# Attention in pairs of heads: row halves for the scores, column halves for the values

## The chip, the cores and the metric

The kernel runs on one core of a Trainium2 chip, in one launch. A core has a matrix engine (TensorE; PE in the profile, its weight loads PEld), a vector engine (VectorE, DVE), a scalar engine (ScalarE, ACT), a general one (GpSimd, POOL) and a queue engine for DMA (SyncE, SP). Each engine works off its own list of instructions in order, and semaphores hold one back until another is done. The metric is the device time of one launch in microseconds, the median of three runs.

## The reference, cut to what matters

Two transformer blocks on 256 tokens of 1024 features, in float32. The first block has two layers, each an attention mixer and a feed-forward part (dense, then eight experts); the second block has one mixer and one feed-forward part. The attention of all four kinds has this core:

```python
s = einsum('hqd,hkd->hqk', q, k) * scale + bias      # scores
m = s.max(-1); e = exp(s - m); den = e.sum(-1)        # softmax; windowed heads add exp(sink - m)
o = einsum('hqk,hkd->hqd', e / den, v)                # values
```

Layer 0 has 8 neighbourhood heads of 64 features (256 latent queries over 512 keys, with a bias; 256 context queries over 256 keys). Layer 1 has 8 windowed heads of 64 (256 queries, 512 keys, two value groups) and 4 differential heads of two halves each. The second block has 4 dilated heads (256 queries, three groups of 256 keys) and 8 MLA heads (96 features for the scores, 64 for the values). Beside layer 0's mixer, modulation vectors are computed: a vector of 1024 times a matrix, for two streams.

## The kernel before, in words

Every matrix of weights streams from HBM and is split by ScalarE (L213) and VectorE (L214) into two parts (`wh`, `wl`), so that a product of full precision is three fast ones (L231 to L233). The attention's own products take float32 operands as they are, and the profile shows each of them as two records.

The program is written out instruction by instruction. A stage's `main` is a generator that issues the projections step by step; each head (or tile of queries of a head) is a task, another generator, with a `yield` after each of its steps. `drive` (L284) sets the order: in a round it issues one step of `main`, starts tasks from `pend` at a rate, lets every live task do one step, and in layer 0 issues `pace` steps of the modulation sums (`ada`, L482: a load of `araw`, then VectorE's L508 or L510 for either stream, and after eight of them TensorE's L522 or L532). A round in which `main` must wait still does the rest. Tiles are shared through `Res` (L62): a task that finds none free yields until one is put back. The eight PSUM banks go through `Bank` (L89), a kind of use each: BG projections, BS scores, BT transposes, BO outputs, with a largest number and a number kept free. So the order on every engine is what these counts make of it.

A task of layer 0 (`head_task`, L785) is one head and one tile t of queries (t 0 and 1 are 128 latent queries each, t 2 both context tiles): load the bias (GpSimd's DMA queue), one score product into a bank (64 rows of the array, the half where the head's features lie), VectorE adds the bias and takes the maximum, ScalarE's Exp sums as it goes, TensorE transposes four blocks of 128, ScalarE or VectorE in turn copies them out, and the value products have the transposed probabilities as stationary side and 64 value columns as moving side, so that the output has tokens on the partitions. When all six tasks of a pair of heads are done, VectorE divides by the denominators and four transposes bring the output to features. The projections of the pairs (`pair_unit`) share two `qkv` tiles (L712): a third pair's projection is copied out (L748) once the first pair's six tasks have ended.

`win_task` (L1319), `dil_task` (L1935) and `mla_task` (L1998) do the same, with one bank for scores (two in `dil_task`) and `merged` (L542) for division and transposes. `diff_task` (L1387) already computes two scores, on the two row halves.

## Time and profile before

| | |
|---|---|
| median of 3 runs | 1788.38 us (1785.85 to 1791.57) |
| span of the profiled execution | 1782.2 us (the profile shows no time outside it; the median lies 6.2 above) |
| TensorE busy | 1686.3 us, 95% |
| weight loads | 1409.1 us, 79% |
| VectorE busy | 1285.6 us, 72% |
| ScalarE busy | 879.4 us, 49% |
| mean granted TensorE clock | 0.984 |
| layer 0's mixer, attention | 108 to 277 us |
| layer 1's mixer, attention | 774 to 877 us |
| second block's mixer, attention | 1414 to 1544 us |

Busy time is the union of the instructions' recorded spans. A product's record includes the latency through the array, which overlaps with the next record; how long it keeps the engine is the distance to the next start.

### The profile page before, as it was taken

To read this page: it belongs to the slowest core of one execution; us is meant where nothing else is said; L and a number is where in the kernel's file an instruction comes from. 1 tells how busy PE (TensorE), PEld (TensorE's weight loads), DVE (VectorE), ACT (ScalarE), POOL (GpSimd) and SP (SyncE) were. 2 spreads that over 40 slices of the span, in tenths; PEclk is the share of its full clock that TensorE was granted. 3 is DMA by queue.
4 is the path that set the end of the run, shared out by engine and by line. 5 is a ranking of instruction groups with operands and counts; after the bars stand their busy time and mean duration, and the time that the engine had idled before them with its cause. 6 is when DMAs were issued, how large, how long until landed. Compare 5 with 4: busy or idle time off the path is not lost. (4 is left out here: it accounts for less than half of the span.)

```text
span 1782.2 us, 23176 instructions
## 1 busy us (share of the span) xinstructions
PE 1686.3 (95%) x8894; PEld 1409.1 (79%) x8894; DVE 1285.6 (72%) x1892; ACT 879.4 (49%) x1326; POOL 75.8 (4%) x149
## 2 busy tenths in 40 slices
PE   5999999999999999999879999999997999979998
PEld 4787877887888887766658888788877999869997
DVE  5788755766765676787879899898996566575555
ACT  6533233522222223435557777777764466545443
POOL 1011100020000000000000000000000000000000
PEclk9998999999999999999999999999998999989999
DMA  8754422473555542343229989898975544246552
GB/s 270 214 163 132 160 71 71 141 204 116 164 181 191 177 142 82 132 142 119 81 80 363 346 298 346 300 359 308 356 233 159 173 131 130 84 141 202 189 189 95
DMA packets 182598, 331.21 MB, mean 186 GB/s; under 512 B 7614, under 2 KB 60192, under 8 KB 182480
## 3 DMA queue, kind: packets, MB, share of 16 engines
q1 hardware_dynamic: 167904, 279.73, 46.1%
q0 software_dynamic: 14576, 49.92, 9.2%
q8 instruction: 72, 1.18, 0.3%
q14 instruction: 46, 0.38, 0.1%
HBM read 328.57 MB, written 1.05 MB: 185 GB/s over the span
## 5 line engine op out<-in xcount | busy, mean ns | idle before, releaser
L214 DVE TENSOR_TENSOR wl<-raw,wh 128x1024 fp32r<-128x1024 f32 (+3 forms) x511 | 570.6, 1145 | 179.8 <-ACT wh L213 177.9
L213 ACT CAST wh<-raw 128x1024 fp32r<-128x1024 f32 (+3 forms) x511 | 489.3, 990 | 285.8 <-PE bank L233 169.7
L231 PE MATMUL bank<-aT,wh 128*128 128x512 f32 (+1 forms) x480 | 186.2, 388 | 1.3 <-DVE aT L435 0.9
L232 PE MATMUL bank<-aT,wh 128*128 128x512 f32 (+1 forms) x480 | 183.1, 381 | 0.8 <-DVE aT L436 0.6
L233 PE MATMUL bank<-aT,wl 128*128 128x512 f32 (+1 forms) x480 | 182.5, 380 | 0.0
L510 DVE SCALAR_TENSOR_TENSOR acc<-araw,sT,acc 128x1024 f32<-128x1024 f32 x105 | 131.1, 1279 | 8.3 <-DMA araw<-in_ada_w_dram 8.1
L231 PE MATMUL bank<-wh,aT 128*128 128x512 f32 (+2 forms) x320 | 119.7, 374 | 5.4 <-DVE aT L435 3.9
L232 PE MATMUL bank<-wl,aT 128*128 128x512 f32 (+2 forms) x320 | 116.8, 365 | 2.8 <-DVE wl L214 2.8
L233 PE MATMUL bank<-wh,aT 128*128 128x512 f32 (+2 forms) x320 | 117.0, 366 | 0.2 <-DVE aT L436 0.2
L232 PE MATMUL bank<-wl,gh 128*128 128x512 f32 (+1 forms) x306 | 114.7, 375 | 2.7 <-DVE wl L214 2.6
L231 PE MATMUL bank<-wh,gh 128*128 128x512 f32 (+1 forms) x306 | 115.7, 378 | 0.0
L233 PE MATMUL bank<-wh,gl 128*128 128x512 f32 (+1 forms) x306 | 114.9, 375 | 0.0
L231 PEld LDWEIGHTS bank<-aT,wh 128*128 128x128 f32 x480 | 90.5, 189 | 23.2 <-ACT P L760 1.5
L232 PEld LDWEIGHTS bank<-aT,wh 128*128 128x128 f32 x480 | 90.6, 189 | 20.5 <-DVE aT L436 1.6
L233 PEld LDWEIGHTS bank<-aT,wl 128*128 128x128 f32 x480 | 90.5, 189 | 19.1
L231 PEld LDWEIGHTS bank<-wh,aT 128*128 128x128 f32 x320 | 61.6, 192 | 16.7 <-DVE aT L435 4.2
L231 PE MATMUL bank<-zT,wh 128*128 128x256 f32 x256 | 71.5, 279 | 0.0
L232 PE MATMUL bank<-zT,wh 128*128 128x256 f32 x256 | 71.3, 279 | 0.0
L233 PE MATMUL bank<-zT,wl 128*128 128x256 f32 x256 | 71.3, 278 | 0.0
L231 PE MATMUL bank<-wh,hidh 128*128 128x512 f32 x176 | 70.0, 398 | 0.0
L233 PE MATMUL bank<-wh,hidl 128*128 128x512 f32 x176 | 69.1, 393 | 0.9 <-DVE hidl L1109 0.9
L232 PEld LDWEIGHTS bank<-wl,aT 128*128 128x128 f32 x320 | 61.5, 192 | 10.5 <-DVE wl L214 3.7
(502 smaller groups left out, 3609.9 us busy)
## 6 DMA issues: line engine op xcount, KB each, us to landing
raw<-in_moe_w_dram SPq DMA_DIRECT2D x96, 1024.0 KB, 7.3
araw<-in_ada_w_dram POOLq DMA_DIRECT2D x80, 512.0 KB, 4.2
raw<-in_moe_w_dram SPq DMA_DIRECT2D x48, 768.0 KB, 5.8
raw<-in_w_ff_dram SPq DMA_DIRECT2D x32, 1024.0 KB, 5.6
raw<-in_ffn_w_dram SPq DMA_DIRECT2D x30, 1024.0 KB, 6.9
raw<-in_ev_w_in_dram SPq DMA_DIRECT2D x48, 256.0 KB, 4.4
raw<-in_w_in_dram SPq DMA_DIRECT2D x10, 1024.0 KB, 5.0
raw<-in_w_in_dram SPq DMA_DIRECT2D x12, 768.0 KB, 4.5
```

Source lines behind the costliest of these rows:

```text
L213: ACT.copy(out=h, in_=v)
L214: DVE.tensor_sub(out=l, in0=v, in1=h)
L231: PE.matmul(o, lt[0], rt[0], start=first, stop=False, skip_group_check=True)
L232: PE.matmul(o, lt[0], rt[1], start=False, stop=False, skip_group_check=True)
L233: PE.matmul(o, lt[1], rt[0], start=False, stop=last, skip_group_check=True)
L510: DVE.scalar_tensor_tensor(acc[s], r, sT[:, s, k:k + 1], acc[s], op0=OP.mult, op1=OP.add)
```

## The change

Two heads make one task. Their two score products are cut into pieces of 256 columns that alternate between the upper and the lower 64 rows (`halves`), into a bank each. For the values, the sides are exchanged: the values (64 columns) are stationary, head 0 on the left half of the columns and head 1 on the right half, and the transposed probabilities stream (`weighted`); the output has features on the partitions, two heads in one bank, and needs no transposes. Since the denominators belong to tokens, `divided` spreads their reciprocals over the features by a product with the identity, after ScalarE has copied the reciprocals out to 512 columns and the output out of its bank, and VectorE multiplies. Tasks take two score banks (four in `dil_task`), two tiles of probabilities and two of their transposes at once; the kept numbers of banks and the rates of `drive` follow; the bias of a pair comes in one load into one tile. `diff_task` uses `halves`. Everything else, the projections, the feed-forward parts and the number of transposes of probabilities among them, stays. (Comments went too; line numbers move by about ten.)

```diff
-    def merged(o, den, BO, rP, BT):
-        """o: two tiles of rows, each of four heads (tokens, (tile, head, 64)), den: their denominators ->
-        a bank of features: ((head, 64) of two heads, (which two, tile, token))"""
-        on = yield from rP.get()
+    def halves(s, q, k, n):
+        for c in range(0, n, 256):
+            for i in range(2):
+                PE.matmul(s[i][:, c:c + 256], q[sl(i, 64)], k[sl(i, 64), c:c + 256], start=True, stop=True)
+    def weighted(o, V, PT, blocks):
+        for n, kt in enumerate(blocks):
+            for i in range(2):
+                PE.matmul(o[sl(i, 64)], V(kt, i), PT(kt, i), start=(n == 0), stop=(n == len(blocks) - 1),
+                          skip_group_check=True)
+    def divided(o, den, y, BO, rP, BT):
+        rd = yield from rP.get()
+        rd = rd[:, 0:512]
         DVE.reciprocal(den, den)
-        DVE.tensor_mul(on[:, :512].rearrange("p (g d) -> p g d", d=64), o.rearrange("p (g d) -> p g d", d=64),
-                       den[:, :, None].to_broadcast([128, 8, 64]))
+        ACT.copy(out=rd.rearrange("p (g d) -> p g d", d=64), in_=den[:, :, None].to_broadcast([128, 8, 64]))
+        ACT.copy(out=y, in_=o)
         BO.put()
         yield
         b = yield from BT.get()
-        for a in range(2):
-            for t in range(2):
-                PE.transpose(b[:, a * 256 + t * 128:][:, :128], on[:, t * 256 + a * 128:][:, :128], ident)
+        for i in range(4):
+            PE.matmul(b[:, sl(i)], rd[:, sl(i)], ident, start=True, stop=True)
         rP.put()
         yield
-        return b
...
-        rP, rPT, rB = (Res(wk, n, k) for n, k in (("P", 4), ("PT", 2), ("bias", 2)))
-        rB.args = ([128, 256], F32)
+        rP, rPT, rB = (Res(wk, n, k) for n, k in (("P", 4), ("PT", 2), ("bias", 1)))
...
+            pend.extend(pair_task(p, t, qkv, QT, KT, ob) for t in range(3))
+        def pair_task(p, t, qkv, QT, KT, ob):
+            ctx_ = t == 2
+            o = yield from shared(ob, 0, BO)
+            if not ctx_:
+                bias = yield from rB.get()
+                bv = bias.rearrange("p (h k) -> p h k", h=2)
+                POOL.dma_start(out=bv, in_=A["rpb_t"][2 * p:2 * p + 2, t].rearrange("h q k -> q h k"))
+                yield
+            den = dens[p].rearrange("p (t h) -> p t h", h=2)
+            nm = yield from rS.get()
+            s = yield from BS.several(2)
+            if ctx_:
+                for i in range(2):
+                    for hh in range(2):
+                        rs = sl(hh, 64)
+                        PE.matmul(s[hh][:, sl(i, 256)], QT[rs, sl(2 + i)], KT[rs, 256:512], start=True, stop=True)
+            else:
+                halves(s, QT[:, sl(t)], KT, 512)
+            yield
+            P = yield from rP.several(2)
             for hh in range(2):
...
+            rS.put()
+            yield
+            PT = yield from rPT.several(2)
+            for hh in range(2):
...
+                return qkv[:, kt, 256 + i * 64:320 + i * 64]
+            if ctx_:
+                weighted(o[:, 256:512], V, lambda kt, i: PT[i][:, sl(kt - 2, 256)], (2, 3))
             else:
...
+                weighted(o[:, sl(t)], V, lambda kt, i: PT[i][:, sl(kt)], range(4))
+            rPT.put(2)
             done[p] += 1
-            if done[p] == 6:
+            if done[p] == 3:
...
+            if done[p] == 3:
...
+                yield from divided(o, dens[p], y32[:, 4 + p, :], BO, rP, BT)
                 done[p] = 7
...
-                    for kind in (BS, BT, BO):
-                        kind.kept = 1
+                    BS.kept, BT.kept, BO.kept = 2, 1, 1
...
-        drive(main, live, pend, rate=1.4, most=8, bgn=pace,
+        drive(main, live, pend, rate=0.7, most=6, bgn=pace,
...
+        BS.kept = 2
...
-            rs = slice(hh * 64, hh * 64 + 64)
+        def win_task(p, t):
+            kv, q = p // 2, p % 2
             ob = yield from shared(state, ("ob", kv), BO)
             nm = yield from rS.get()
-            nm = nm.rearrange("p a b -> p (a b)")[:, 0:1]
-            i = t * 4 + hd % 4
-            den, es = wden[kv][:, 0, i:i + 1], wden[kv][:, 1, i:i + 1]
-            s = yield from BS.get()
-            PE.matmul(s, cQT[rs, p, sl(t)], cKT[rs, kv, :], start=True, stop=True)
-            yield
-            P = yield from rP.get()
+            nm = nm.rearrange("p a b -> p (a b)")
+            i = (q * 2 + t) * 2
+            den, es = (wden[kv][:, k, i:i + 2] for k in range(2))
+            s = yield from BS.several(2)
+            halves(s, cQT[:, p, sl(t)], cKT[:, kv, :], 512)
+            yield
...
-            rPT.put()
+            PT = yield from rPT.several(2)
+            for hh in range(2):
+                yield from turned_probs(P[hh], rP, PT[hh])
+            weighted(ob[:, sl(q * 2 + t)], lambda kt, i: ckv[:, kt, 128 + kv * 64:192 + kv * 64],
+                     lambda kt, i: PT[i][:, sl(kt)], range(4))
+            rPT.put(2)
...
             s0, s1 = yield from BS.several(2)
-            for i, s in enumerate((s0, s1)):
-                PE.matmul(s, dQT[sl(i, 64), hd, sl(t)], dKT[sl(i, 64), :], start=True, stop=True)
+            halves((s0, s1), dQT[:, hd, sl(t)], dKT, 512)
...
+        BS.kept = 4
...
+            s0 = yield from BS.several(4)
+            s0, s1 = s0[0:2], s0[2:4]
             for g in range(3):
...
+                halves([x[:, 0:256] for x in s1] if g == 2 else [x[:, sl(g, 256)] for x in s0],
+                       QK[0][:, 2 * g + jp, sl(t)], QK[1][:, 2 * g + jp, :], 256)
...
+            P = yield from rP.several(2)
...
+            weighted(ob[:, sl(jp * 2 + t)], lambda k, i: va[:, k % 2, (4 * (k // 2) + 2 * jp + i) * 64:][:, :64],
+                     lambda k, i: PT[i][:, sl(k)], range(6))
+            rPT.put(2)
             flags["dil"] += 1
-            if flags["dil"] == 8:
+            if flags["dil"] == 4:
+                BS.kept = 2
...
+            s = yield from BS.several(2)
             for t in range(2):
-                PE.matmul(s[:, sl(t, 256)], Q[:, hd, sl(t)], K[:, hd, :], start=True, stop=True)
-            yield
```

The order that comes of it, at two places of layer 0. First TensorE in the first stretch in which no projection can be issued, before: L798 and L801 are scores (latent and context), L820 and L823 transposes of probabilities, L834 values, L776 transposes of the next pair's queries and keys.

```order
L798 MATMUL bank<-KT,QT 128x512
L834 MATMUL bank<-qkv,PT 128x64 x4
L820 MATMUL bank<-ident,P 128x128 x4
L823 MATMUL bank<-ident,P 128x128 x4
L834 MATMUL bank<-qkv,PT 128x64 x4
L776 MATMUL bank<-ident,qkv 128x128 x4
L820 MATMUL bank<-ident,P 128x128 x4
L834 MATMUL bank<-qkv,PT 128x64 x8
L820 MATMUL bank<-ident,P 128x128 x4
L801 MATMUL bank<-KT,QT 128x256 x2
L834 MATMUL bank<-qkv,PT 128x64 x4
L798 MATMUL bank<-KT,QT 128x512
```

And now: L547 and L813 are scores, L841 and L843 transposes of probabilities, L553 values, L790 the next pair's, L522 column sums of the modulation.

```order
L843 MATMUL bank<-ident,P 128x128 x4
L522 MATMUL bank<-acc,ones 128x512
L843 MATMUL bank<-ident,P 128x128 x4
L522 MATMUL bank<-acc,ones 128x512
L790 MATMUL bank<-ident,qkv 128x128 x4
L813 MATMUL bank<-KT,QT 128x256 x4
L553 MATMUL bank<-PT,qkv 64x128 x8
L547 MATMUL bank<-KT,QT 128x256 x4
L841 MATMUL bank<-ident,P 128x128 x8
L553 MATMUL bank<-PT,qkv 64x256 x4
L843 MATMUL bank<-ident,P 128x128 x8
L553 MATMUL bank<-PT,qkv 64x128 x8
```

Before, six heads' scores, transposes and values stand mixed; now one pair's steps follow each other, with little of another task between.

VectorE in the same stretch, before: L805 and L806 are a head's bias and maximum, L810 the context maximum, L508 and L510 the modulation sums, L54 copies of transposes and, last, of the third pair's projection.

```order
L805 TENSOR_TENSOR bank<-bank,bias 128x256
L806 TENSOR_REDUCE ast<-bank 128x1
L508 TENSOR_SCALAR acc<-araw,sT 128x1024
L54 COPY PT<-bank 128x512
L54 COPY KT<-bank 128x512
L510 SCALAR_TENSOR_TENSOR acc<-araw,sT,acc 128x1024 x4
L54 COPY PT<-bank 128x512
L510 SCALAR_TENSOR_TENSOR acc<-araw,sT,acc 128x1024 x2
L810 TENSOR_REDUCE ast<-bank 128x2
L510 SCALAR_TENSOR_TENSOR acc<-araw,sT,acc 128x1024 x2
L54 COPY qkv<-bank 128x384
```

And now (L826, L827 and L821 in their place):

```order
L821 TENSOR_REDUCE ast<-bank 128x2 x2
L510 SCALAR_TENSOR_TENSOR acc<-araw,sT,acc 128x1024 x2
L826 TENSOR_TENSOR bank<-bank,bias 128x256
L827 TENSOR_REDUCE ast<-bank 128x1
L826 TENSOR_TENSOR bank<-bank,bias 128x256
L827 TENSOR_REDUCE ast<-bank 128x1
L510 SCALAR_TENSOR_TENSOR acc<-araw,sT,acc 128x1024 x4
L54 COPY PT<-bank 128x512
L510 SCALAR_TENSOR_TENSOR acc<-araw,sT,acc 128x1024 x5
L54 COPY PT<-bank 128x512
L510 SCALAR_TENSOR_TENSOR acc<-araw,sT,acc 128x1024 x3
L54 COPY qkv<-bank 128x384
```

From the last L508 to the copy of the projection there were eight L510; now there are fourteen, in runs of up to five between two copies of probabilities.

The second place is the end of the fourth pair's projection, TensorE, before, where the second pair's last values lie between projection products:

```order
L232 MATMUL bank<-wl,aT 128x384
L233 MATMUL bank<-wh,aT 128x384
L834 MATMUL bank<-qkv,PT 128x64 x4
L231 MATMUL bank<-wh,aT 128x384
L232 MATMUL bank<-wl,aT 128x384
L233 MATMUL bank<-wh,aT 128x384
```

And now, between two projections, where L532 are column sums of the modulation:

```order
L553 MATMUL bank<-PT,qkv 64x256 x4
L843 MATMUL bank<-ident,P 128x128 x8
L553 MATMUL bank<-PT,qkv 64x128 x8
L843 MATMUL bank<-ident,P 128x128 x4
L532 MATMUL bank<-ones,acc 128x1 x8
L843 MATMUL bank<-ident,P 128x128 x4
L532 MATMUL bank<-ones,acc 128x1 x8
L553 MATMUL bank<-PT,qkv 64x128 x8
```

The context values, the transposes and values of two tiles of queries and both column sums now stand together, with no projection between; on VectorE six L510 stand between that pair's last maximum and its copies.

## Rows read from the trace of the kernel before

**Rows 1.** The page, part 1: busy us, share of the span, instructions
```profile
PE 1686.3 (95%) x8894; PEld 1409.1 (79%) x8894; DVE 1285.6 (72%) x1892; ACT 879.4 (49%) x1326; POOL 75.8 (4%) x149
```

**Rows 2.** Windows (us): length, then each engine's busy us; clock, DMA share, GB/s
```profile
121.00:145.00 24.00, 23.14 (x109) 14.59 (x108) 20.70 (x27) 7.42 (x20) 3.73 (x7) 0.85 0.40 120
...
813.00:877.00 64.00, 56.11 (x353) 39.42 (x352) 48.53 (x121) 32.68 (x87) 0.53 (x1) 1.00 0.25 87
...
1413.00:1544.00 131.00, 127.71 (x926) 117.83 (x925) 79.18 (x152) 79.08 (x163) 0.00 (x0) 1.00 0.35 112
```

**Rows 3.** Timeline, TensorE, a projection: start, us, engine, line, operands, count
```profile
1543.64 0.28 PE L232 MATMUL bank<-ya,wh 128*128 128x256 f32 x1
...
1543.76 0.28 PE L233 MATMUL bank<-ya,wl 128*128 128x256 f32 x1
```

**Rows 4.** Timeline, TensorE: score products and what follows
```profile
828.77 1.12 PE L1328 MATMUL bank<-ck,X 64*128 64x512 f32 x2
...
829.83 1.09 PE L1310 MATMUL bank<-ident,P 128*128 128x128 f32 x8
...
851.01 1.13 PE L1394 MATMUL bank<-raw,X 64*128 64x512 f32 x4
...
1459.21 1.56 PE L1945 MATMUL bank<-QK 64*128 64x256 f32 x6
```

**Rows 5.** Timeline, TensorE: value products, transposes and what follows
```profile
1451.99 1.45 PE L1961 MATMUL bank<-va,PT 128*128 128x64 f32 x12
...
1537.99 1.00 PE L2019 MATMUL bank<-h,PT 128*128 128x64 f32 x8
...
1538.83 0.61 PE L1927 MATMUL bank<-ident,P 128*128 128x128 f32 x4
...
856.32 1.06 PE L1415 MATMUL bank<-h,PT 128*128 128x128 f32 x8
```

**Rows 6.** By source line: count, ns min/median/max, first and last start
```profile
L834 PE MATMUL bank<-qkv,PT x192: 217/275/421, 128.0 to 275.6; 128*128 128x64 f32 x192
...
L1328 PE MATMUL bank<-ck,X x32: 589/589/693, 774.4 to 834.4; 64*128 64x512 f32 x32
```

**Rows 7.** Timeline of layer 0's first attention stretch, VectorE and TensorE
```profile
128.56 0.43 DVE L805 TENSOR_TENSOR bank<-bank,bias 128x256 f32<-128x256 f32 x1
...
129.02 0.69 DVE L806 TENSOR_REDUCE ast<-bank 128x1 f32<-128x512 f32 x1
...
132.09 4.86 DVE L510 SCALAR_TENSOR_TENSOR acc<-araw,sT,acc 128x1024 f32<-128x1024 f32 x4
...
142.85 0.56 DVE L54 COPY qkv<-bank 128x384 f32<-128x384 f32 x1
...
144.71 0.79 PE L231 MATMUL bank<-aT,wh 128*128 128x512 f32 x1
```

**Rows 8.** Copies by source line (as rows 6), and column sums in the timeline
```profile
L54 DVE COPY PT<-bank x35: 417/683/693, 126.7 to 1539.5; 128x512 f32<-128x512 f32 x27, 128x256 f32<-128x256 f32 x8
...
L54 DVE COPY qkv<-bank x4: 557/557/558, 72.6 to 194.8; 128x384 f32<-128x384 f32 x4
...
L52 ACT COPY PT<-bank x37: 571/584/607, 124.8 to 1538.2; 128x512 f32<-128x512 f32 x37
...
178.16 1.84 PE L532 MATMUL bank<-ones,acc 128*128 128x1 f32 x16
```

**Rows 9.** DMA issues: tile, queue, count, KB each, median us to landing
```profile
araw<-in_ada_w_dram POOLq DMA_DIRECT2D x80, 512.0 KB, 4.2
...
bias<-in_rpb_t_dram POOLq DMA_DIRECT2D x16, 128.0 KB, 4.0
```

**Rows 10.** Timeline, TensorE: ends of the three attention stretches
```profile
277.05 0.48 PE L231 MATMUL bank<-wh,aT 128*128 128x512 f32 x1
...
876.17 0.66 PE L1435 MATMUL bank<-ident,PT 128*128 128x128 f32 x4 [1.43 <-DVE PT L1431]
...
1543.03 0.66 PE L554 MATMUL bank<-ident,P 128*128 128x128 f32 x4 [1.47 <-DVE P L547]
```

More of the change, by code (lines that the diff above doesn't have):

```diff
@@ L815, in head_task @@
             rS.put()
             yield
-            b = yield from BT.get()
-            for i in range(4):
-                if t < 2:
-                    PE.transpose(b[:, sl(i)], P[:, sl(i)], ident)
-                else:
-                    kt, q = divmod(i, 2)
-                    PE.transpose(b[:, sl(i)], P[:, q * 256 + kt * 128:q * 256 + (kt + 1) * 128], ident)
-            rP.put()
-            yield
-            PT = yield from rPT.get()
-            cp(flip(), PT, b)
-            BT.put()
@@ L837, in head_task @@
-            rPT.put()
+            PT = yield from rPT.several(2)
+            for hh in range(2):
+                b = yield from BT.get()
+                for i in range(4):
+                    if ctx_:
+                        kt, q = divmod(i, 2)
+                        PE.transpose(b[:, sl(i)], P[hh][:, q * 256 + kt * 128:q * 256 + (kt + 1) * 128], ident)
+                    else:
+                        PE.transpose(b[:, sl(i)], P[hh][:, sl(i)], ident)
+                rP.put()
+                yield
+                cp(flip(), PT[hh], b)
+                BT.put()
@@ L843, in head_task @@
                 yield
-                on = yield from rP.get()
-                rd = dens[p].rearrange("p t h -> p (t h)")
-                DVE.reciprocal(rd, rd)
-                DVE.tensor_mul(on.rearrange("p (g d) -> p g d", d=64), o.rearrange("p (g d) -> p g d", d=64),
-                               rd[:, :, None].to_broadcast([128, 8, 64]))
-                BO.put()
-                yield
-                b = yield from BT.get()
-                for i in range(4):
-                    PE.transpose(b[:, sl(i)], on[:, sl(i)], ident)
-                rP.put()
-                yield
-                ACT.copy(out=y32[:, 4 + p, :], in_=b)
-                BT.put()
+                yield from divided(o, dens[p], y32[:, 4 + p, :], BO, rP, BT)
                 done[p] = 7
@@ L1274, in ck_prep @@
                 yield
-            pend.extend(win_task(hd, t) for hd in range(8) for t in range(2))
+            pend.extend(win_task(p, t) for p in range(4) for t in range(2))
         def q_prep(x, gi, QT, then):
@@ L1312, in turned_probs @@
             yield
[L1313 removed]
+            if PT is None:
+                PT = yield from rPT.get()
             cp(flip(), PT, b)
@@ L1338, in win_task @@
+            BS.put(2)
+            DVE.tensor_add(nm[:, 2:4], nm[:, 0:2], sink[:, 2 * p:2 * p + 2])
+            ACT.activation(out=es, in_=nm[:, 2:4], func=AF.Exp)
             rS.put()
             yield
-            PT = yield from turned_probs(P, rP)
-            for kt in range(4):
-                PE.matmul(ob[:, sl(i, 64)], PT[:, sl(kt)], ckv[:, kt, 128 + kv * 64:192 + kv * 64],
-                          start=(kt == 0), stop=(kt == 3), skip_group_check=True)
-            rPT.put()
+            PT = yield from rPT.several(2)
@@ L1920, in probs_T @@
         def probs_T(P, blocks):
[L1922 to L1924 removed]
+            PT = yield from rPT.several(2)
+            todo = [(i, k, b) for i in range(2) for k, b in enumerate(blocks)]
+            for n0 in range(0, len(todo), 4):
                 b = yield from BT.get()
[L1926 to L1927 removed]
+                for n, (i, _, c) in enumerate(todo[n0:n0 + 4]):
+                    PE.transpose(b[:, sl(n)], P[i][:, sl(c)], ident)
@@ L1954, in dil_task @@
-            ACT.activation(out=P[:, 512:768], in_=s1[:, 0:256], func=AF.Exp, bias=nm[:, 0:1], accum_out=den[:, 1])
-            BS.put(2)
+            P = yield from rP.several(2)
+            for hh in range(2):
+                n2 = nm[:, 2 * hh:2 * hh + 2]
+                DVE.tensor_add(s0[hh], s0[hh], dm[:, t, 0:512])
+                DVE.reduce_max(out=n2[:, 0:1], in_=s0[hh], axis=AX, negate=True)
+                DVE.tensor_add(s1[hh][:, 0:256], s1[hh][:, 0:256], dm[:, t, 512:768])
+                DVE.reduce_max(out=n2[:, 1:2], in_=s1[hh][:, 0:256], axis=AX, negate=True)
+                DVE.tensor_tensor(out=n2[:, 0:1], in0=n2[:, 0:1], in1=n2[:, 1:2], op=OP.min)
+                ACT.activation(out=P[hh][:, 0:512], in_=s0[hh], func=AF.Exp, bias=n2[:, 0:1],
+                               accum_out=den[:, 0, hh:hh + 1])
+                ACT.activation(out=P[hh][:, 512:768], in_=s1[hh][:, 0:256], func=AF.Exp, bias=n2[:, 0:1],
+                               accum_out=den[:, 1, hh:hh + 1])
@@ L1956, in dil_task @@
+            BS.put(4)
             rS.put()
```

184 lines of the change are left out of this document (73 added, 111 removed).

## The prediction

> **What bounds the kernel now.** I read the page's busy shares first, then one table of windows over the three mixers (the only stages with attention), then single stretches of the timeline. The page gives TensorE 95% of the span [rows 1], but that is made of latencies that overlap: in a projection, products recorded as 0.28 us each start 0.12 us apart [rows 3]. So a change is priced by the distance from one start to the next, not by busy time. TensorE has work almost without a break in all three mixers; VectorE is at 86% in the first mixer's attention stretch at 121 to 145 us, 76% in layer 1's attention at 813 to 877 and 60% in the second block's mixer [rows 2]. So TensorE time saved in the second block should arrive at the end, and in the first two mixers VectorE and the chains score, softmax, transpose, copy, values stand ready to take its place.
>
> **The change part by part, on TensorE.** *Scores.* A single head's score product of 512 columns holds TensorE from 828.77 to 829.83, 1.06 us [rows 4]. The differential heads of this same kernel already send two heads, on the two row halves, one behind the other: four records in 1.13 us where one head has two in 1.12 [rows 4]. So a pair costs what a head costs. Layer 0 goes from 24 score calls to 12 (the context ones, two products of 256 columns, cost the same), the windowed heads from 16 to 8: 20 x 1.06 = 21.2 us saved. A dilated head's six records take 1.56 us, of which 0.07 is the tail that the next work overlaps: 1.49, and four calls fewer save 6.0. Cutting 512 columns into two of 256 is priced at nothing: the bits streamed are the same, and the second weight load lies beside a running product, as in the dilated scores, which already have 256 columns. The MLA scores have 96 rows and stay as they are. Sum -27.2.
>
> *Values.* Before, the probabilities are stationary (128 columns) and 64 columns stream: a head has 8 records and holds TensorE 0.84 us (1537.99 to 1538.83), a dilated one 12 records in 1.45 less the tail of 0.16, 1.3 [rows 5]; layer 0 alone has 192 such records [rows 6]. After, the values are stationary and 128 probability columns stream, in 16 records a pair. No row shows two column halves of the array at work, so I bound it from both sides. A record of 128 columns has a pace of 0.11 us (eight transposes recorded in 1.06 us, 0.90 without the tail of 0.16: 0.90/8) [rows 5]. If the halves run together as the row halves do, a pair takes 0.90, and 0.2 for going in and out of the split array (1.06 of a score call less two streams of 0.43): 1.10 against 1.68, 0.58 saved. If they run one after the other, 1.80 + 0.2 = 2.0: 0.32 lost. For a dilated pair that is 0.95 saved (1.35 + 0.2 against 2.5) or 0.4 lost, for an MLA pair 0.62 saved (1.06 against 1.68) or 0.24 lost. With 20, 4 and 4 pairs: -17.9 together, +9.0 one after the other. I take together, by the nearest row, the row halves, and keep the other end as a rival.
>
> *Dividing.* Nine groups of four transposes (0.61 us recorded, 0.5 without the tail [rows 5]) become nine of four full products of 128 columns, two records each, 0.90: +3.6. Each has two ScalarE copies in front (0.58 each [rows 8]) and VectorE's multiplication behind; in the middle of a stage other tasks cover them, at the end of one they are exposed.
>
> TensorE thus has 27.2 + 17.9 - 3.6 = 41.5 us less: layer 0 18.1, layer 1 12.3, second block 11.1.
>
> **What of it is given back.** *Layer 0, first stretch.* The third pair's projection cannot be copied out until the first pair is done with its memory, so TensorE has attention alone until 144.71, and VectorE copies that projection at 142.85 [rows 7]. Meanwhile every round also issues modulation sums (L510), 1.22 us each in a row (four in 4.86 [rows 7]). VectorE's list from the first gate addition to that copy has 8 of them before and 14 now, and one softmax of a head less (0.43 + 0.69 [rows 7]) and one of a context head less (0.69): 6 x 1.22 - 1.8 = +5.5 on the busiest engine of the stretch, less the two score calls (2.1) by which it starts earlier and some 2 us in which VectorE idled; and TensorE's column sums (16 records, 1.84 us [rows 8]) now stand ahead of the next projection. I put its resumption 2 us later than before, where TensorE alone would have been 5 earlier; the seven loads of 4.2 us [rows 9] into three `araw` buffers, with so many L510 in a row, can add 0 to 4. The bias has one tile for a pair now; its load (4.0 us for one head [rows 9]) waits for the addition of the pair before and stands in POOL's queue behind those loads. The next addition lies far enough behind, but for the last pair's: priced at nothing, 0 to 4 there.
>
> *Second stretch.* From there to the fourth pair's copy by VectorE at 194.8 [rows 8] were 50.1 us. TensorE's list between these points has seven value calls, three groups of transposes and one column sum less, a score call more and a dearer division: 7 x 0.84 + 3 x 0.5 + 1.84 - 1.06 - 0.4 = 7.7 less, since the second pair's heads have hardly begun. Before, those were all done when the copy came; now it waits for them. The last softmax of that pair (2.2), then six L510 (7.3), then a copy of probabilities (0.68 [rows 8]) make 10 us on VectorE, with 6 us of TensorE work beside them; after them come two value calls, transposes and two column sums, 7 us. TensorE resumes at about 146.7 + 42.4 + 4 + 7 + 2 for the copies between = 202 instead of 194.7: 8 late with what I round off.
>
> *Rest of layer 0.* From 194.7 to the output projection's second half at 277.05 [rows 10] it took 82.3. Six score and six value calls become cheaper and three divisions dearer: 6 x 1.06 + 6 x 0.58 - 1.2 = 8.6 less, 73.7. The two score banks now hold one pair, so that four times a score call waits for the softmax of the pair before, 2 to 4 us each where no projection lies between; 11 in all, of which 6 stood there before in other waits: 78.7, 3.6 earlier. And two column sums that came after the stage are already done, 3.6. Layer 0 ends 8 - 3.6 - 3.6 = 1 later, 3 with the loads: all 18.1 and 3 more are given back (bounds: 9 earlier, 10 later).
>
> *Layer 1.* From 813 the heads run alone. TensorE has full work to the last windowed score at 834.4 [rows 6], then chains, down to the transposes at 876.17 that wait 1.43 us for VectorE [rows 10]. The pairs gain in the first part; the chains at the end stay, and 48.5 us of VectorE work in 64 [rows 2] do not shrink. Of 12.3 I give back 7: -5.3.
>
> *Second block.* Dilated pairs lie between projections: 6.0 + 3.8 - 0.4 = -9.4. The MLA heads' end at 1543 is a chain that already waits 1.47 [rows 10]; the pair's coarser step and the two copies cost 2 there, so that what MLA saves goes. -9 (bounds -11 and -2).
>
> Sum: +3 - 5.3 - 9 = -11.3 on the span of 1782.2. The median of the runs is 6.2 above that span, for what lies around it and does not change: 1788.4 - 11.3 = 1777.
>
> **Rivals.** *A, column halves one after the other.* For it: no row of this kernel shows them together, and both halves read all 128 rows. Against it: the row halves do. Price 17.9 + 9.0 = 26.9 us of TensorE; 7 of layer 0's 10.8 (the rest falls beside VectorE's stretches), 5 of layer 1's 7.2 and 8 of the second block's 8.9 arrive: +20, 1797, slower. It decides as soon as a pair's 16 records take 1.8 us or more.
> The Trainium skill ("TensorE: Matmul & The Clock Gate", Part 3) says that weight loads lie beside running products only where their row groups differ, which speaks against column halves; the same part reports three column tiles at 2.38 times the speed of one. By the first a pair would come near A; by the second I estimate 1.1 to 1.4 us a pair and some 3 us less gain than I forecast. In this trace the weights of full-height products are loaded at the full pace (L1415, 128 columns in 0.11 us), so the first is not borne out here.
> *B, TensorE's gain arrives whole or nearly.* For it: almost no idle time of TensorE in the second block. Against it: VectorE's lists of layer 0. With 30 of the 41.5 arriving: 1758.
> *C, pairs wait for pairs.* The place is layer 1's stretch: three score banks hold one pair, so a pair's scores wait for both softmaxes of the one before. For it: per pair VectorE has two additions, two maxima and a copy, about 2.9 us, and ScalarE behind it, 4.6 in a chain, against 3.1 on TensorE. Against it: the bank limit rises to four there. Five pairs x 1.5, and 3 at each of the two other ends: +11 on my forecast, 1788, no change.
>
> **How the numbers follow.** Forecast 0.47 (its own range 1768 to 1786), A 0.20, B 0.15, C 0.18. What a measurement can tell is about 0.3%, 5.4 us. Faster than 1783: 0.41 of the forecast, B whole, 0.03 of C: 0.59. Slower than 1793.8: 0.17 of A, 0.05 of C: 0.22. The rest, 0.19, is no change. The range 1756 to 1799 leaves out B's and A's far ends.
>
> **What would show it.** Right: a pair's score products as four (256 columns: eight) records, starting two at a time, within 1.1 us; a pair's 16 value records in 1.1; TensorE idle, waiting for L510 and for copies behind it, at 125 to 145 and near 190 to 200; layer 0's output projection beginning at 277 give or take 5; the second block's mixer 9 shorter. Wrong: value records 0.11 apart one by one (A); those two stretches of layer 0 shorter than before (B); gaps of 1.5 us before each windowed pair's scores (C). A half-clock stretch longer than the present one (0.85 of 2.4 GHz granted on average over 121 to 145 [rows 2], so part of it at 1.2 GHz) would be a loss that I have not priced.

## The result, and the profile after

The changed kernel takes 1804.68 us (median of 4 runs, 1803.92 to 1805.86) against 1788.8 us before (median of 4): 1.0083 times the time before, 95% interval 1.0067 to 1.0098. It is slower by 16 us, and lies almost 6 us beyond the end of the predicted range, 1799. The profiled execution has a span of 1803.4 us and a granted TensorE clock of 0.968 on average; before it was 1782.2 us and 0.984. The kernel before took from 1782 us (granted clock 0.984) to 1794 us (0.978) in its runs beside the experiments, so the execution in its profile is one of its quickest, and the table below measures from that one.

The page's first part, TensorE busy 9 us less in a span 21 us longer [rows 1]:

```profile
PE 1677.5 (93%) x8962; PEld 1402.2 (78%) x8962; DVE 1286.9 (71%) x1900; ACT 881.1 (49%) x1330; POOL 73.1 (4%) x141
```

Windows of the same kernel (length, busy us of TensorE, its weight loads, VectorE, ScalarE, GpSimd, then the clock):

```profile
121.00:145.00 24.00, 14.78 (x81) 8.96 (x80) 23.92 (x28) 5.00 (x16) 3.71 (x7) 0.65 0.53 157
196.00:216.00 20.00, 14.70 (x76) 13.55 (x77) 7.30 (x10) 2.87 (x6) 0.00 (x0) 0.51 0.04 16
814.00:821.00 7.00, 4.77 (x13) 3.35 (x14) 6.72 (x16) 3.07 (x7) 0.00 (x0) 0.51 0.00 0
...
1428.00:1560.00 132.00, 122.18 (x879) 106.34 (x877) 77.47 (x147) 75.51 (x161) 0.00 (x0) 0.96 0.35 111
```

In layer 0's first stretch VectorE is busy for 23.92 of 24 us (20.70 before) and TensorE for 14.78 (23.14 before) [rows 2]; the clock is 0.65 there, 0.51 at 196 to 216, and 0.96 in the second block's mixer, where it was 1.00.

The products themselves do what was forecast. TensorE in layer 1, a pair's values and a pair's scores:

```profile
826.53 1.23 PE L553 MATMUL bank<-PT,ck 128*64 128x128 f32 x16
827.69 1.14 PE L547 MATMUL bank<-ck,X 64*128 64x256 f32 x8
```

Sixteen value records of 128 columns hold TensorE for 1.16 us (from 826.53 to 827.69); one after the other they would need 16 x 0.11 [rows 5]. So where did the time go? The same projection product (counted from the first; every kernel has 2312 in L231) starts later than in the profiled execution before by so many us (a minus: earlier). This table is worked out from the traces; the columns are the product's start in the kernel before, and e2 to e12 are the experiments below:

| kernel | 106 | 150 | 219 | 322 | 743 | 813 | 936 | 1412 | 1544 | 1774 |
|---|---|---|---|---|---|---|---|---|---|---|
| changed | -0.4 | +3.7 | +17.3 | +9.9 | +9.8 | +11.8 | +15.7 | +14.9 | +19.5 | +21.2 |
| e2 | -1.0 | +2.9 | +16.3 | +8.8 | +10.0 | +2.4 | +14.4 | +13.6 | +13.1 | +13.1 |
| e3 | +0.5 | -11.5 | -12.4 | -0.2 | +0.7 | +2.1 | +4.9 | +4.8 | +9.6 | +11.1 |
| e5 | +3.1 | -8.2 | -5.0 | -5.6 | -4.4 | -3.8 | +0.3 | -0.5 | +3.8 | +6.0 |
| e6 | +3.5 | -7.7 | -4.5 | -6.1 | -4.2 | -11.8 | -0.7 | -0.7 | +0.4 | +2.4 |
| e7 | +4.9 | -5.1 | -1.9 | -3.6 | -3.5 | -0.3 | +0.8 | +0.2 | -0.3 | +1.2 |
| e8 | +4.1 | +13.4 | +13.5 | +12.3 | +13.1 | +17.7 | +18.8 | +17.9 | +18.8 | +20.5 |
| e9 | 0.0 | -10.8 | -6.6 | -9.1 | -7.6 | -14.2 | -3.2 | -3.3 | -8.9 | -6.9 |
| e10 | -0.6 | +3.3 | +12.8 | +7.7 | +9.6 | +11.4 | +15.4 | +14.5 | +19.0 | +20.2 |
| e12 | -1.0 | -11.8 | -7.5 | -10.0 | -8.5 | -3.5 | -2.5 | -3.3 | -9.4 | -7.6 |

Layer 0's mixer ends 9.9 late, layer 1's adds 5.9 (743 to 936), the second block's 4.6 (1412 to 1544).

Layer 0, VectorE in the first stretch (start, us, line; what answers to [rows 7]):

```profile
130.45 4.86 DVE L510 SCALAR_TENSOR_TENSOR acc<-araw,sT,acc 128x1024 f32<-128x1024 f32 x4
135.23 0.69 DVE L54 COPY PT<-bank 128x512 f32<-128x512 f32 x1
135.83 6.06 DVE L510 SCALAR_TENSOR_TENSOR acc<-araw,sT,acc 128x1024 f32<-128x1024 f32 x5
141.80 0.69 DVE L54 COPY PT<-bank 128x512 f32<-128x512 f32 x1
142.40 3.67 DVE L510 SCALAR_TENSOR_TENSOR acc<-araw,sT,acc 128x1024 f32<-128x1024 f32 x3
145.99 0.56 DVE L54 COPY qkv<-bank 128x384 f32<-128x384 f32 x1
```

and TensorE's first projection product behind it:

```profile
148.43 0.77 PE L231 MATMUL bank<-aT,wh 128*128 128x512 f32 x1
```

Each copy of probabilities stands behind four to five sums, and the qkv copy comes at 145.99 instead of 142.85. The second stretch, VectorE and then TensorE:

```profile
193.39 7.25 DVE L510 SCALAR_TENSOR_TENSOR acc<-araw,sT,acc 128x1024 f32<-128x1024 f32 x6
200.56 0.68 DVE L54 COPY PT<-bank 128x512 f32<-128x512 f32 x1
...
213.63 0.56 DVE L54 COPY qkv<-bank 128x384 f32<-128x384 f32 x1 [1.67 <-PE bank L553]
```

```profile
195.01 0.43 PE L553 MATMUL bank<-PT,qkv 128*64 128x128 f32 x2
201.30 1.97 PE L553 MATMUL bank<-PT,qkv 128*64 128x128 f32 x14 [5.86 <-DVE PT L54]
203.20 1.12 PE L843 MATMUL bank<-ident,P 128*128 128x128 f32 x4
204.11 3.41 PE L532 MATMUL bank<-ones,acc 128*128 128x1 f32 x16
...
211.61 1.97 PE L553 MATMUL bank<-PT,qkv 128*64 128x128 f32 x16
```

TensorE waits 5.86 us for the copy behind six sums. What follows runs at half the clock: column sums of 3.41 us that took 1.84 [rows 8], values of 1.97 us. The copy of the fourth pair's projection comes at 213.63, and came at 194.8 [rows 8]. The last projection product ahead of this wait still starts 2.8 us earlier than before (191.28, before 194.09), the next one 18.9 later (213.52, before 194.61).

Layer 1 and the second block, TensorE, scores of a pair:

```profile
816.23 2.07 PE L547 MATMUL bank<-ck,X 64*128 64x256 f32 x6 [5.67 <-ACT P L1344]
```

```profile
1448.99 0.70 PE L547 MATMUL bank<-QK 64*128 64x256 f32 x2
1453.33 2.08 PE L547 MATMUL bank<-QK 64*128 64x256 f32 x8 [3.64 <-ACT P L1969]
1455.65 1.22 PE L547 MATMUL bank<-QK 64*128 64x256 f32 x2 [0.25 <-ACT P L1969]
```

They wait for Exp of the pair before to leave the bank, with projections queued behind them; and there too the records that follow take nearly twice their time (eight in 2.08 us, where 1.14 is shown above).

The second block's mixer as a whole, between the products of 1412 and 1544, before and now:

```profile
1411.77:1543.88 132.11, 128.82 (x930) 118.73 (x928) 79.44 (x152) 80.19 (x165) 0.00 (x0) 1.00 0.35 115
```

```profile
1426.71:1563.40 136.69, 126.72 (x909) 110.13 (x908) 78.75 (x150) 79.26 (x168) 0.00 (x0) 0.96 0.35 111
```

TensorE runs no product for 10.0 us, where it was 3.3.

### The profile page after: what moved, and what is told of

Its sections match the earlier page's. It is cut to its first block, busy times and chain, and to the rows that moved or that the text cites. A ratio compares the mean times of both kernels' runs of the same rounds, so it can differ in the third digit from the quotient of the medians.

```text
span 1803.4 us, 23332 instructions
## 1 busy us (share of the span) xinstructions
PE 1677.5 (93%) x8962; PEld 1402.2 (78%) x8962; DVE 1286.9 (71%) x1900; ACT 881.1 (49%) x1330; POOL 73.1 (4%) x141
## 5 line engine op out<-in xcount | busy, mean ns | idle before, releaser
L231 PE MATMUL bank<-aT,wh 128*128 128x512 f32 (+1 forms) x480 | 186.9, 389 | 0.9 <-DVE aT L435 0.9
L510 DVE SCALAR_TENSOR_TENSOR acc<-araw,sT,acc 128x1024 f32<-128x1024 f32 x105 | 130.7, 1281 | 9.5 <-DMA araw<-in_ada_w_dram 9.3
L231 PE MATMUL bank<-wh,aT 128*128 128x512 f32 (+2 forms) x320 | 119.5, 373 | 5.5 <-DVE aT L435 3.9
L231 PE MATMUL bank<-wh,gh 128*128 128x512 f32 (+1 forms) x306 | 115.7, 378 | 0.0
L231 PEld LDWEIGHTS bank<-aT,wh 128*128 128x128 f32 x480 | 90.9, 189 | 21.6 <-issue 2.0
L231 PEld LDWEIGHTS bank<-wh,aT 128*128 128x128 f32 x320 | 61.7, 193 | 15.5 <-DVE aT L435 4.2
L231 PE MATMUL bank<-zT,wh 128*128 128x256 f32 x256 | 71.3, 279 | 0.0
L231 PE MATMUL bank<-wh,hidh 128*128 128x512 f32 x176 | 70.2, 399 | 0.0
```

The costliest lines, as they stand in the source:

```text
L231: PE.matmul(o, lt[0], rt[0], start=first, stop=False, skip_group_check=True)
L510: DVE.scalar_tensor_tensor(acc[s], r, sT[:, s, k:k + 1], acc[s], op0=OP.mult, op1=OP.add)
```

## The experiments

Theories: sums in VectorE's list hold TensorE up in layer 0; score products wait in TensorE's list for the banks of the pair before; and each such wait costs again, since the clock is at half behind it. Medians of different experiments were not all taken side by side; each ratio is to the kernel before, with its 95% interval.

**e1_by_head**: the column halves without turns.

```diff
-        for n, kt in enumerate(blocks):
-            for i in range(2):
+        for i in range(2):
+            for n, kt in enumerate(blocks):
```

> The changed kernel with one edit: the value products of a pair go head by head (all blocks of the left column half, then all of the right) instead of in turns. Nothing is left out. Theory 1 (two column halves work together when their products alternate, which is why a pair's 16 records take 1.1 us in the changed kernel): now the 16 records follow each other at 0.11 us, 1.8 us and 0.2 for entering, so a call of 16 takes about 2.0 instead of 1.16; over 20 calls of a window's or a neighbourhood head, 4 dilated and 4 of 8 records about 24 us more of TensorE work, of which 10 to 24 should arrive in the time. Theory 2 (the halves never overlap, rival A of the prediction): the same time as the changed kernel, within 2 us, and the same spacing of the records.

1807.19 us, 1.0111 (1.0076 to 1.0146), not told apart from the changed kernel's 1.0083; of the 10 to 24 us of theory 1, 2.5 came by the medians. A dilated pair's 24 records, in the changed kernel and in this one:

```profile
1479.91 1.53 PE L553 MATMUL bank<-PT,va 128*64 128x128 f32 x24
```

```profile
1481.44 2.46 PE L553 MATMUL bank<-PT,va 128*64 128x128 f32 x24
```

So the turns are worth 0.9 us in such a call, and rival A has fallen: in turns the halves run together. My price for head by head was too high, since they still overlap: where a call runs without a stop, the 16 records of a pair start within 1.31 us, not 15 x 0.11 = 1.65, and within 0.82 in turns.

**e2_late_banks**: in the dilated pairs, and likewise in the windowed ones.

```diff
-            BS.put(4)
             rS.put()
             yield
+            BS.put(4)
```

> The changed kernel with one edit, in the windowed and the dilated pairs only: a pair gives its score banks back one step later, so that the next pair's score products stand at least one step of projections further down in TensorE's list. Nothing is left out. Theory 1 (score products of a pair wait in TensorE's list for the softmax of the pair before, with projections stuck behind them): the waits before L547 of 5.7 us at 816 and 3.6 at 1453 go or fall under 1 us, and the half-clock stretches behind them too; 4 to 10 us faster than the changed kernel. Theory 2 (the loss there comes from tasks that take probabilities and transposed tiles two at a time, not from the banks): the waits move to other lines, and the time stays within 2 us of the changed kernel or gets worse.

1798.3 us, 1.0066 (1.0042 to 1.0091): 6 us faster than the changed kernel by the medians, though the intervals overlap; e6 against e5, below, shows the same 6. The wait of 5.67 is gone, that of 3.64 is 1.10, and the product of 813 starts at +2.4 instead of +11.8; but layer 1 ends at +14.4, and the rest is given back where attention runs alone (813 to 879). The second block's mixer goes from 4.6 longer to 0.5 shorter. Theory 1 holds for the waits, and for the end only in the second block.

**e3_sums_wait**: no sums while a qkv tile is awaited.

```diff
-            qkv = yield from rQKV.get()
+            while rQKV.free == 0:
+                hold[0] = True
+                yield
+            hold[0] = False
+            qkv = rQKV.now()
...
             for s in segs:
+                while any(hold):
+                    yield True
```

> The changed kernel with one edit in layer 0: no modulation sum is issued while the program waits for a qkv tile or, as before, for layer 0's last divisions; those that began keep their turn. Nothing is left out; the sums come later. Theory 1 (the sums in VectorE's list between a pair's softmax and its copies hold TensorE up in both stretches): the third pair's projection is copied out near 138 instead of 146 us, the fourth's near 200 instead of 213.6; some 2 to 6 us come back where the sums are done later, so 6 to 14 us faster than the changed kernel. Theory 2 (all sums have to be done before layer 0 ends, so their place doesn't matter): the two stretches get shorter, and the end of layer 0, at about 300 to 310 us, waits for them by as much; within 3 us of the changed kernel.

1795.18 us, 1.0039 (1.0022 to 1.0057), 9.5 us faster than the changed kernel by the medians, inside theory 1's 6 to 14. The two stretches end at -11.5 and -12.4, where the changed kernel had +3.7 and +17.3. Then 12.2 us come back: VectorE at layer 0's end still has sums to do, and what waits for them:

```profile
294.68 7.26 DVE L514 SCALAR_TENSOR_TENSOR acc<-araw,sT,acc 128x1024 f32<-128x1024 f32 x6
307.82 0.24 DVE L540 TENSOR_TENSOR mod<-bank,vec 128x8 f32<-128x8 f32 x2 [5.88 <-PE bank L536]
```

```profile
300.80 6.99 PE L536 MATMUL bank<-ones,acc 128*128 128x1 f32 x32 [6.81 <-DVE acc L514]
```

Both theories are right in part: the place cost the time, and the number left for the end cost some again.

**e4_fill**: 132 useless transposes into the bank that the next real ones overwrite.

```diff
                 b = yield from BT.get()
+                for i in range({(0, 2, 1): 56, (0, 1, 1): 28, (1, 1, 1): 48}.get((p, t, hh), 0)):
+                    PE.transpose(b[:, sl(i % 4)], ident, ident)
```

> The changed kernel with useless work added: 132 transposes of the identity, overwritten afterwards, in three places of layer 0 where TensorE waits for VectorE (56 and 28 at 128 to 142 us, 48 at 194 to 200), about 14.5 us of TensorE work. Theory 1 (waiting makes the granted clock fall to half, and the work behind the waits runs at half pace: 201 to 214 us took 12.3 us, of which I put 5.5 down to the clock, and 136 to 151 about 4): the clock stays at full in these stretches, transposes behind them take 1.05 us for eight and not 1.97, and the kernel gets 4 to 9 us faster though it does more. Theory 2 (the half clock costs nothing, because VectorE sets the pace there): the same time or up to 3 us slower.

1804.22 us, 1.0098 (1.0059 to 1.0137): no change, so the forecast of 4 to 9 failed. The clock was 0.94 at 120 to 152 (0.63 in the changed kernel), but the first fillers delayed real transposes: the product of 150 starts at +6.2 instead of +3.7.

**e10_fill_second**: only the 48 of the second stretch.

> The changed kernel with useless work in one place only: 48 transposes of the identity, overwritten afterwards, ahead of the last transposes in the wait of 194 to 200 us (in e4_fill this stretch got 5.7 us shorter, but the fillers of the first stretch stood where they held up the transposes, and took 2.3 us of it back). Theory 1 (half clock behind a wait is a cost of its own): 3 to 6 us faster than the changed kernel. Theory 2 (what is won there is waited for later, by VectorE's work of the last pairs): within 1.5 us of the changed kernel.

1803.02 us, 1.0066 (1.0049 to 1.0082). Here the stretch shows what half clock costs; TensorE, with L839 the fillers:

```profile
193.45 5.40 PE L839 MATMUL bank<-ident 128*128 128x128 f32 x48
...
200.91 1.09 PE L553 MATMUL bank<-PT,qkv 128*64 128x128 f32 x14 [1.25 <-DVE PT L54]
201.92 0.66 PE L845 MATMUL bank<-ident,P 128*128 128x128 f32 x4
202.42 1.84 PE L532 MATMUL bank<-ones,acc 128*128 128x1 f32 x16
...
206.66 1.97 PE L553 MATMUL bank<-PT,qkv 128*64 128x128 f32 x16
```

From the value records behind the copy to the last ones' start it took 5.8 us (200.91 to 206.66) instead of 10.3 (201.30 to 211.61). Between the products of 194 and 219 it gained 4.1 us; about 2 of them are left at 322 and none at 743. The whole time is inconclusive: 1.7 us less than the changed kernel by the medians, with intervals that overlap, where theory 1 had 3 to 6. So the half clock costs 4 to 5 us in the stretch, and no run shows that they arrive at the end.

**e5_sums_spread**: e3, and `pace = [2.6]`.

> The changed kernel with the edit of e3_sums_wait and one number more: the sums' rate outside the waits is 2.6 a step instead of 1.8, so that in VectorE's list all 48 of them stand ahead of layer 0's last normalisation, as in the kernel before. Nothing is left out. In e3 the two stretches ended 15 and 30 us earlier than in the changed kernel, and 16.5 us were lost again where layer 0's end waited for the last sums. Theory 1 (that wait was only a matter of too few sums between the stretches): it goes, at most 6 us come back in VectorE's fuller list between 150 and 240, and the kernel gets 8 to 14 us faster than e3 (1781 to 1787). Theory 2 (VectorE has no room for them there either): the loss moves into the projections of 150 to 240 and the time is that of e3 within 3 us.

1790.4 us, 1.0008 (0.9994 to 1.0023): not told apart from the kernel before. By the medians it is 5 us faster than e3, less than the 8 to 14 expected. Layer 0 now ends 5.6 ahead of the kernel before (changed kernel: 9.9 behind).

**e6_sums_banks**: e5 and e2.

> The edits of e5_sums_spread and e2_late_banks together. Nothing is left out. If they act in different stages and add up, e2's 6 us come off e5's time: 1775 to 1781, faster than the kernel before. If layer 1 and the second block only passed on a lateness that began in layer 0, e6 equals e5 within 2 us.

1784.32 us, 0.9978 (0.9959 to 0.9996). Taken beside e5 it is 6.1 us faster by the medians: the two edits add up, as expected. The range of 1775 to 1781 was missed, because e5 itself came out slower than expected.

**e7_old_layer1**: e6 with layer 1's single heads.

> As e6_sums_banks, but layer 1 has the single heads of the kernel before (scores of 512 columns, values by token, division and transposes). Nothing is left out. Theory 1 (in layer 1 the pairs cost more in waits for VectorE and ScalarE than TensorE gains, 4.7 us between 743 and 923 in e2): 3 to 6 us faster than e6. Theory 2 (the pairs are worth their 5 us there and the loss seen in the changed kernel comes from clock stretches that the late banks removed): 1 to 6 us slower than e6.

1784.28 us, 0.9965 (0.9951 to 0.9979), equal to e6: both theories fail, in layer 1 it makes no difference.

**e8_before_sums**: the kernel before with e5's edit.

> The kernel before (single heads everywhere) with the edit of e5_sums_spread alone: no modulation sum is issued while the program waits for a qkv tile, rate 2.6 otherwise. Nothing is left out. Theory 1 (the sums held up the kernel before too: eight of them stand between the second copies and the third pair's projection, and 138 to 148 us ran at half clock): 4 to 9 us faster than before. Theory 2 (only the pairs suffered from them): the same within 2 us, so that what e5 gains over the changed kernel is all owed to the pairs.

1799.86 us (ten runs, 1794.09 to 1806.91; the profiled one took 1804.49), 1.006 (1.0036 to 1.0084): slower, which neither theory had. TensorE's only wait in that stretch, and the window of 132 to 162 behind it:

```profile
128.48 1.12 PE L806 MATMUL bank<-KT,QT 64*128 64x512 f32 x2 [1.09 <-ACT P L815]
```

```profile
132.00:162.00 30.00, 30.00 (x99) 21.93 (x99) 10.61 (x17) 8.93 (x23) 1.80 (x4) 0.51 0.04 11
```

TensorE has work in all of the 30 us and VectorE in a third of them, yet the clock stays at half (0.51). Between the products of 106 and 150 the kernel loses 9.3 us in this way, with TensorE without a product for 1.1 us (0.9 before). So what the pairs gain by this edit isn't something that the kernel before left lying.

**e9_spread**: e6, with the rate raised only after the first wait, and a dilated pair's banks given back after its transposes.

```diff
-            hold[0] = False
+            if hold[0]:
+                hold[0], pace[0] = False, 2.6
...
-            BS.put(4)
             PT = yield from probs_T(P, range(6))
+            BS.put(4)
```

> The edits of e6_sums_banks with two changes of place: the sums' rate rises to 2.6 only after the first wait for a qkv tile (in e6 the denser sums cost 3.5 us ahead of 106 us), and a dilated pair gives its score banks back after its own transposes, so that the four pairs' scores stand 28 and 48 projection products apart instead of 12 to 48 (in e6 the third pair's scores still waited for softmaxes at about 1437 to 1441, with a half-clock stretch behind). Nothing is left out. Theory 1 (what still eats the pairs' gain are waits in TensorE's list): layer 0 ends 8 to 11 us ahead of the kernel before instead of 6, the second block's mixer gets 3 to 6 us shorter than in e6: 1776 to 1780. Theory 2 (the gain in the second block goes to VectorE and the end chain whatever the order): the mixer stays at e6's length, and only layer 0 gives 2 to 4 us: 1780 to 1783.

1776.14 us, 0.9916 (0.9899 to 0.9932): faster than both kernels, and as theory 1 had it. Windows of the two stretches:

```profile
120.00:152.00 32.00, 29.52 (x169) 20.77 (x168) 22.30 (x40) 11.43 (x31) 1.84 (x3) 0.95 0.29 84
190.00:218.00 28.00, 26.83 (x129) 20.20 (x129) 25.57 (x41) 13.20 (x29) 3.37 (x6) 1.00 0.40 122
```

VectorE is at 70% in the first (22.30 of 32 us) instead of 91% in the changed kernel (29.08), and the clock at 0.95 and 1.00 instead of 0.63 in either. The dilated pairs' waits for banks are gone; layer 0 ends at -9.1, and the second block's mixer is 5.6 shorter than before.

**e11_wide_scores**: one product of 512 columns per head.

> The changed kernel with one edit: a pair's score products are one of 512 columns per head, as the differential heads had them before, instead of two of 256 in turns. Nothing is left out. By the prediction the pieces cost nothing: a call of 4 records takes 1.06 to 1.13 us like the 8 now, and the time is the same within 2 us. The rival: the alternation of pieces is what lets the row halves run together, and the call takes 2 us; then 8 to 20 us slower.

1808.32 us, 1.0102 (1.0085 to 1.0119), against the changed kernel's 1.0083 (1.0067 to 1.0098): by the medians 3.6 us slower, more than the 2 allowed for, but the intervals overlap. The rival's 8 to 20 did not come. A call of four records is recorded as 1.13 us, as with eight; cutting the products changes nothing in them, as predicted.

**e12_spread_old_l1**: e9 with layer 1's single heads.

> As e9_spread, but layer 1 has the single heads of the kernel before. Nothing is left out. Theory 1 (in layer 1 the pairs gain 10 us beside the projections and give them back in the stretch where attention runs alone, which is a chain through VectorE and ScalarE; e6 and e7 were equal): within 2 us of e9, 1774 to 1778. Theory 2 (e7's old layer 1 only had a half-clock stretch at 802 that it needn't have, and the kernel before had none there): 3 to 5 us faster than e9, 1771 to 1773.

1776.12 us, 0.9921 (0.9904 to 0.9937), e9's time, as theory 1 had it. The pairs of e9 are 10.6 us ahead of these single heads at the product of 813 and less than 1 ahead at 936.

## Why the prediction was wrong

The forecast added +3 for layer 0, -5.3 for layer 1 and -9 for the second block; the traces have +9.9, +5.9 and +4.6, and 0.8 elsewhere. Layer 0 lies just inside its bounds (10 later), the second block far outside its own (-11 and -2), and layer 1 had none. Of the signs named, the records of scores and values and the idle stretches of layer 0 came; layer 0's output projection (second half) began at 291.0 and not at 277 give or take 5, and the second block's mixer got longer.

**TensorE's work: right.** A score call of a pair 1.1 us, a value call 1.16 where I took 1.10, the column halves together. Rival A had a chance of 0.20 and fell by the first row of values. The rule of the Trainium skill ("TensorE: Matmul & The Clock Gate", Part 3) that speaks against column halves isn't borne out here; my estimate from the same part, 1.1 to 1.4 us a pair, holds the measured 1.16 (826.53 to 827.69).

**Layer 0's first stretch: right in mechanism, too small in size.** TensorE resumed at 148.43 (144.71 before [rows 7]): 3.7 late, not 2. The loads that could add 0 to 4 don't show: VectorE is busy for 23.92 of 24 us.

**Layer 0's second stretch: this term failed in size.** I had it 8 late; the qkv copy came 18.8 late. I had 7 us of TensorE work behind VectorE's copies, at full clock. It took 12.3 (201.30 to 213.63), at half. The last line of the forecast named a longer half-clock stretch as a loss that it had not priced; e10 prices it: 4 to 5 us of this stretch, though what it saved here did not last to the product of 743. Most of the rest is there before the wait: TensorE reached it at 195.4 (195.01 + 0.43), where I had 189. The first stretch's 1.7 and the half clock that lasts until 152 are part of that; the wait itself took 5.86 where I had 4. From this copy to layer 0's end 8.9 us came back (18.8 to 9.9), and I had 7.2. In sum +9.9 where the forecast had +3.

**Second block: this step failed.** "Dilated pairs lie between projections", with -9.4, treated them as filler that TensorE can always run. I put pairs that wait for pairs into the rest of layer 0 and into rival C, there mainly into layer 1, and did not see that a pair's four banks are handed on as soon as its softmax is issued, not done, so that the next scores stand in TensorE's list at once. The second block's -9 became +4.6, 13.6 off. TensorE has 6.7 us more without a product there than before (10.0 against 3.3), 3.64 of them in the wait at 1453, and a clock of 0.96 over 136.7 us costs some 5 more (an estimate from these two numbers): together about 12. With the banks given back one step later (e2) the mixer is at -0.5, with the pairs spread (e9) at -5.6. In e9 it is -10.9 up to the product of 1498, more than I had forecast; from there the MLA heads' end gives 5.3 back, where I had 2.

**Layer 1: failed in part, and part is not the pairs'.** The wait of 5.67 at 816 is rival C's mechanism in its place. But taking it away moves nothing at the end: in e9 the pairs are 6.6 ahead between 743 and 813 and lose 11.0 from there to 879, where attention runs alone. There TensorE has 12.3 us without a product (7.9 before) and a clock of 0.89 (1.00 before); that it is the chains through VectorE and ScalarE that decide is my reading, and no run takes them apart. I gave back 7 of 12.3, a figure that I had no row for; all of it goes, since single heads make e12 as fast as e9. Against the profiled execution before, layer 1 is 3.5 to 6 us late in every kernel whose layer 0 was changed, with its own single heads too (e7 +4.3, e8 +5.7, e12 +6.0). The code of layer 1 is the same in the kernel before and in e8; between the products of 743 and 813, before and then in e8:

```profile
742.97:812.66 69.69, 64.63 (x282) 48.42 (x281) 61.32 (x136) 25.25 (x42) 5.22 (x11) 1.00 0.39 128
```

```profile
756.03:830.35 74.32, 69.28 (x282) 52.34 (x281) 62.21 (x136) 25.23 (x42) 5.22 (x11) 0.93 0.39 123
```

The records are as many, and TensorE is without a product for 5.1 and 5.0 us; the clock is 0.93 instead of 1.00, and the stretch takes 4.6 us longer. So most of what layer 1 adds to the changed kernel is not shown to be owed to the pairs. What decides whether such a half-clock stretch comes (e7, e8 and e12 have one near 800 to 820) is left open.

**The baseline.** I put the 6.2 us between span and median down to what lies around the span. The profiled execution after has a span of 1803.4 us and a run of 1805.17: 1.8 around it. So the execution before that I read was some 4.4 us faster than its kernel's median, about as much as the half clock costs in layer 1 above; that it is the same loss is not shown. It is why 21.2 us of difference in spans are 16 in the medians.

**Rivals.** B was out of reach with this order of work. C had the right mechanism, too small a place and no clock. Its sum was wrong too: five pairs at 1.5 and 3 at each of two ends are 13.5, not 11. None of the cases put together the waits of two stages and the clock behind them.

That e9's 1776 is near the 1777 forecast does not make the forecast right: it is another order of work, with other gains in each stage.

## What to carry to other kernels

When work is merged into coarser tasks, look at what stands between a task's steps in the lists of the other engines, and at how early a resource counts as free: a bank handed on when its last reader is issued puts a wait into an in-order list, with everything behind it. Price a wait of the matrix engine twice where the granted clock falls behind it, once as time and once as the half clock, which made 5.8 us of work into 10.3 here; and ask whether the gain arrives, since of what e10 saved in its stretch nothing was left at the product of 743. Compare a profiled execution with the median of its own runs before reading differences of a few microseconds. Here the change took 0.8% off the time only after the sums and the banks were moved with it.

## What the runs showed of the hardware

- Two column halves of the array run side by side in float32: 24 records in 1.53 us in turns, 2.46 head by head, and even then the second head's records begin before the first's have ended.
- A granted clock of half can stay for 30 us in which TensorE waits for nothing (e8, 132 to 162, 0.51); it rose to full at about 161.5, after projections had resumed at 158.20. The Trainium skill ("TensorE: Matmul & The Clock Gate", Part 1) says that half rate is the resting state and activity ends it; the clock of 0.51 behind the wait of 5.86 agrees with that, but busy time as the profile records it (30.00 of 30.00 us in e8) did not end it.
- The same 282 records of TensorE, with the same time without a product, took 69.69 us at a granted clock of 1.00 and 74.32 at 0.93 (kernel before and e8).
- Useless transposes in a wait (48 in 5.40 us) kept the clock up, and the needed work right behind them went at its full pace (column sums 1.84 us instead of 3.41).
